# A decoder trunk in fp32 on one core: the query and key projections that fill the attention stage go chunk by chunk to one PSUM bank at a time

## Chip, cores and metric

One core of a Trainium2 chip runs the kernel. The metric is the device time of one execution in microseconds (us). The median of 3 runs counts.

## What is computed

A trunk of two layers is applied to 1024 prompt tokens and 8 sample tokens (T = 1032 columns; model width 1024). Layer 0 mixes with a recurrent block (RG-LRU), layer 1 with sliding-window attention; behind each mixer stands a squared-ReLU MLP. The change lies in the attention of layer 1. Cut to that, the reference reads:

```python
q, k, v = jnp.split(x @ w_qkv, [Q_DIM, Q_DIM + KV_DIM], axis=-1)
q = rms_norm(q.reshape(n, t, N_KV, GROUP, HEAD_DIM), q_g)     # 16 query heads of 64
k = rms_norm(k.reshape(n, t, N_KV, HEAD_DIM), k_g)            # 4 key heads of 64
...
s = jnp.einsum('...qkgd,...skd->...kgqs', q, k).astype(jnp.float32) * (HEAD_DIM ** -0.5)
s = s - alibi_slopes()[:, :, None, None] * dist.astype(jnp.float32)
s = jnp.where(mask, s, NEG_INF)                               # window of 128
m = jnp.maximum(jnp.max(s, axis=-1, keepdims=True), sink)
e = jnp.exp(s - m)
p = e / (jnp.sum(e, axis=-1, keepdims=True) + jnp.exp(sink - m))
return jnp.einsum('...kgqs,...skd->...qkgd', p.astype(v.dtype), v)
```

## The kernel before, in words

Every large product is made of three passes over split operands (`passes`, L235): high part by high part, high by low, low by high, all added up in PSUM. Activations lie with the model width on the 128 partitions, as eight tiles of 1032 columns; `hs[k]` is the pair (`hh`, `hl`) of tile k.

The program runs through the recurrent block, the first MLP, the attention, and the second MLP. In the attention stage (1039.5 to about 1260 us of the trace) the work is written as a loop of NJ = 64 steps j, each one pair of heads' tile t (8 of them) and one block b of 128 queries (8 of them). A step has these parts:

- `stage_a(j)`, called two steps ahead: POOL builds two bias tiles (L955), PE makes four score matmuls into a bank `S` (L961), DVE the masked minimum (L965, twice), ACT the exponentials (L968, twice), DVE the reciprocals (L970), POOL the scaling (L973, twice).
- `stage_b(j)`: PE transposes the probabilities into the bank `T` (L983, up to four), and ACT or DVE, by turns, copies them to `pt` (L988).
- `stage_c(k)`, every fourth step: 28 or 32 matmuls of probabilities by values into the bank `O` (L1005), which ACT and DVE copy out.

These parts leave PE idle, so a generator, `filler` (L1100), puts pieces of other products between them: `take(n)` runs n pieces. The pieces are the query projections t = 1 to 7, with the projection of the second key tile ahead of t = 4, and after step J0 = 52 the output projection. Weights of the next projection are split into `wh` (ACT, L185) and `wl` (DVE, L186) when a projection starts. PSUM has 8 banks: one `N`, three `P`, two `S`, one `T`, one `O`.

A projection has three chunks of columns: 384, 384 and 264 for a query tile, three times 344 for a key tile. In `proj_steps` (L877) all three chunks are summed side by side, in the three `P` banks. A piece is one pass of one of the eight `k`, so three matmuls with the same weights, one to each bank: 24 pieces. Then comes a piece in which all three banks are taken out, and three pieces with the statistics, one for each chunk. These four have no matmul of a projection. So a projection has 28 pieces, and the eight of them 224.

Taking out a chunk of queries is `q_take` (L798): ACT squares it (L805) and writes the high part `hi` (L806), DVE writes the low part `lo` (L807), and SP starts four DMAs to the tiles `q0` and `q1` that the scores read. `q_stats` (L819) makes the sums of squares: 16 small matmuls into bank `N` (L829), a copy by ACT (L832), two transposes (L836), and the factors (L791 to L796); it acts when it is called with the third chunk. For the key tile it is `take_out` (L764) and `k_evac` (L854), which holds the norm (`qk_norm`, with one matmul into `N`, L773) and the split.

The order is that of the calls, as each engine runs its instructions in the order in which they were issued to it. Some matmuls are tied to their place by `issue_after`. `T0 = 24` pieces are taken ahead of the loop, 7 behind each of the first two `stage_a`, then TF = 3.6 in each step on average (three or four) up to step 52. `done` holds the projections that are finished; the loop takes pieces until the tile that `stage_a` needs is in it. From step 46 on `split_o` splits the attention's results into `oh` and `ol` (L276, L277), in tiles that earlier held `hh` and `hl`, and `ensure` splits the first weights of the output projection. At the end of the stage the output projection's `entry_steps` adds the residual on DVE (`y`, L384), starts a DMA from ACT (L385), and scales (L387).

Of the kernel before, what the change touches and what calls it, by code (L numbers as in the profile page):

```python
# [16 lines left out]
P = 128  # L17
D = 1024
M8 = D // P
# [4 lines left out]
NCH = 3  # L24
# [10 lines left out]
KCOLS = [slice(c * CH, (c + 1) * CH) for c in range(NCH)]  # L35
QCOLS = [slice(0, 3 * P), slice(3 * P, 6 * P), slice(6 * P, T)]
# [28 lines left out]
def trunk(ctx: ExitStack, tc: tile.TileContext, I, O):  # L65
# [48 lines left out]
    def B(tag=None):  # L114
        if tag is None:
            tag = ring[turn[0] % len(ring)]
            turn[0] += 1
        return psum["pool"].tile([P, 512], F32, tag=tag, bufs=BANKS[tag], name=nm("b" + tag))
# [11 lines left out]
    def r_(x):  # L130
        return x.bitcast(F32R)
# [103 lines left out]
    def passes(w, x):  # L235
        (wh, wl), (xh, xl) = w, x
        return ((wh, xh), (wh, xl), (wl, xh))
# [508 lines left out]
    def attention(hs):  # L746
# [72 lines left out]
        def q_stats(t, c, s):  # L819
            stq.setdefault(t, []).append(s)  # L820
            if c < 2:
                return
            st, ss, chain = B("N"), stq.pop(t), last.get("values")
            for b in (6, 7, 0, 1, 2, 3, 4, 5):
                r, j = divmod(b, 4)
                with ExitStack() as x:
                    if chain:
                        x.enter_context(tc.issue_after(chain))
                    chain = pe.matmul(st[32 * j:32 * j + 32, r * P:r * P + P], lhsT=blk[:, 0:P:4], rhs=ss[b // 3][:, b % 3 * P:b % 3 * P + P],  # L829
                                      start=True, stop=True).ins  # L830
            sb = S("sts", 256)
            act.copy(sb, st[:, 0:256])  # L832

            def rest():
                for r in range(2):
                    pe.transpose(st[:, 256 + r * P:256 + r * P + P], sb[:, r * P:r * P + P], ident)  # L836
                sums = st[:, 256:512].rearrange("p (b x) -> p b x", x=32)[:, :, 0:32:16]
                y, x, q = (fac[t % 3][:, 2 * NB * k:2 * NB * k + 2 * NB].rearrange("p (b u) -> p b u", u=2) for k in range(3))
                factors_of(y, x, sums, q)

            if t:
                rest()
            return rest

        stats0 = []

        def q_evac(t, c, ps):
            s = q_take(t, c, ps)
# [17 lines left out]
                    for half in (lower, upper):  # L866
                        sp.dma_start(kst[p][u][n][half, cs(c)], x[own, :])

        done = {("q", 0), ("k", 0)}

        def after_values():
            s = ExitStack()
# [1 line left out]
                s.enter_context(tc.issue_after(last["values"]))  # L874
            return s

        def proj_steps(tag, w, cols, take, evac):  # L877
            ps = [B("P")[:, :sl.stop - sl.start] for sl in cols]
            for k in range(M8):
                for a, (wt, xt) in enumerate(passes(w, hs[k])):  # L880
                    for c, sl in enumerate(cols):
                        with after_values():
                            last["mm"] = pe.matmul(ps[c], lhsT=r_(wt[:, k * P:k * P + P]), rhs=r_(xt[:, sl]),  # L883
                                      start=(k == 0 and a == 0), stop=(k == M8 - 1 and a == 2)).ins
                    yield
            sx = [take(c, o) for c, o in enumerate(ps)]
            yield
            for c in range(NCH):
                evac(c, sx[c])
                yield  # L890
            done.add(tag)

        v_tiles = [W("v") for _ in range(2)]
        vnew = tc.dram_tile([2, D], F32, name="vnew")
# [205 lines left out]
        def filler():  # L1100
            for t in range(1, 8):
                if t == 4:
                    yield from proj_steps(("k", 1), unit("k", 1, 1), KCOLS, lambda c, o: take_out(o), lambda *a: k_evac(1, *a))
                yield from proj_steps(("q", t), unit("q", t, 1 if t < 7 else 0), QCOLS, lambda *a, t=t: q_take(t, *a),
                                      lambda *a, t=t: q_stats(t, *a))

        def split_o(t, sl):
            if t not in ohl:
# [19 lines left out]
        def take(n):  # L1128
            for _ in range(n):
                next(fill, None)  # L1130

        NJ = 8 * NB
        WHEN = (44, 47, 49, 54, 60)
        AHEAD, T0, T1, TF, J0, JS = 2, 24, 7, 3.6, 52, 46
        take(T0)
        for j in range(AHEAD):
            stage_a(j)
# [1 line left out]
        for j in range(NJ):  # L1139
            if j + AHEAD < NJ:  # L1140
                while ("q", STEPS[j + AHEAD][0]) not in done:
                    take(1)
                stage_a(j + AHEAD)
            if j == J0:
                run(fill)
                xs, need, grow, fill = out_proj("wo1", srcs, spill, "g_mlp1", None, spill1, before=between, after=ahead(1), early=WAVE)
            if JS <= j < JS + 6:
                split_o(j - JS, cs(0))
            if j in WHEN:
                ensure(index["wo1", WHEN.index(j)])  # L1150
            if j == J0 + 5:
                grow(2)
            if J0 + 4 <= j < J0 + 7:
                split_o(j - J0 - 4, slice(CH, SEQ))
            n = int((j + 1) * TF) - int(j * TF) if j < J0 else 3 if j < J0 + 8 else 4
            take(n // 2)
            if j % 4 == 0 and j > 0:
                stage_c(j // 4 - 1)
            stage_b(j)
            take(n - n // 2)  # L1160
        take(4)
        stage_c(NJ // 4 - 1)
        for t in range(3, 6):
# [417 lines left out]
```

## Time and profile before

| | |
|---|---|
| times of three runs | 2006.60, 2006.76, 2008.14 us; median 2006.76 us |
| the profiled execution | 2005.53 us, of which the span of the trace is 2003.3 us |
| granted TensorE clock, mean | 0.996 |
| busy share of the span | PE 99%, DVE 69%, ACT 52%, POOL 19% |
| matmuls | 15452 |

The profile is of one execution. A row of the windows view gives a stretch of the span, its length, the busy time of each engine in it with the number of instructions that started there, the clock that TensorE was granted (1.00 is full speed), and how busy the DMA engines were. A row of the timeline is an instruction or a run of like ones: start, duration, engine, line, operation, `out<-in`, and in square brackets how long the engine was idle ahead of it and whose instruction released it. A row of the waits view sums such idle times for a pair: the total, how often, and the longest. PE is TensorE, DVE the vector engine, ACT the scalar engine, POOL is GpSimd; names of tiles begin with b for PSUM banks (`bP`, `bS`).

### The profile page before, as it was taken

What the parts mean: (1) busy time and instruction counts of PE and PEld (TensorE: products, weight loads), DVE (VectorE), ACT (ScalarE), POOL (GpSimd) and SP (SyncE); (2) the same over time, 40 slices, a digit from 0 to 9 for tenths busy, and PEclk for the clock granted to TensorE, in tenths of its full rate; (3) what the DMA queues carried; (4) which work ended last, traced back from release to release, by engine and by line L of the source; (5) the groups of instructions that cost most, each with busy time, mean ns of one, the idle gap of its engine ahead of it and who ended that gap; (6) DMA issues with size and microseconds to landing.
All of it is one profiled execution on the core that took longest, in us unless ns stands there. A gap on an engine that the chain in (4) does not pass through costs nothing.

```text
span 2003.3 us, 39287 instructions
## 1 busy us (share of the span) xinstructions
PE 1985.7 (99%) x15452; PEld 1955.7 (98%) x15452; DVE 1385.8 (69%) x2515; ACT 1050.4 (52%) x2049; POOL 373.0 (19%) x688
## 2 busy tenths in 40 slices
PE   9999999999999999999999989999999999999999
PEld 9999999999999999999999979999999999999999
DVE  7986639866676876766746657578766668776673
ACT  8786436444344655545446656455444446554551
POOL 2230100000002133312006657000000002332220
PEclk9999999999999999999999999999999999999999
DMA  5112422434346688769332323623443446877775
GB/s 175 49 43 64 145 82 71 162 130 160 132 148 236 168 231 239 213 164 216 113 100 73 90 70 102 216 82 112 143 154 134 158 138 198 239 208 185 211 194 133
DMA packets 110856, 294.40 MB, mean 147 GB/s; under 512 B 18488, under 2 KB 43328, under 8 KB 110672
## 3 DMA queue, kind: packets, MB, share of 16 engines
q1 hardware_dynamic: 53712, 125.82, 20.4%
q0 software_dynamic: 29024, 97.85, 19.0%
q10 hardware_dynamic: 27936, 68.23, 9.4%
q8 instruction: 121, 1.98, 0.4%
q14 instruction: 63, 0.52, 0.1%
HBM read 170.97 MB, written 108.19 MB: 139 GB/s over the span
## 4 chain that ended last, share of the span: by engine, by line
PE 96%; DMA 1%; DVE 1%; ACT 1%; issue 1%; POOL 0%; ACTq 0%; SPq 0%; DVEq 0%; POOLq 0%
PE bD L557 61%; PE bP L245 11%; PE bS L245 7%; PE bP L883 4%; PE bO L245 3%; PE bT L245 3%; PE bO L1005 1%; PE bS L961 1%; PE bT L983 1%; PE bS L906 1%; DMA tl<-hsum 1%; ACT se L968 0%; DMA spill<-y 0%; PE bN L829 0%; DMA x<-xT 0%
## 5 line engine op out<-in xcount | busy, mean ns | idle before, releaser
L557 PE MATMUL bD<-op,op 128*128 128x258 f32 x5544 | 678.7, 283 | 0.0
L557 PEld LDWEIGHTS bD<-op,op 128*128 128x128 f32 x5544 | 671.2, 189 | 5.0 <-ACT ho L692 4.5
L557 PE MATMUL bD<-tl,op 128*128 128x258 f32 x4704 | 579.6, 284 | 0.3 <-DVE ho L696 0.3
L557 PEld LDWEIGHTS bD<-tl,op 128*128 128x128 f32 x4704 | 570.2, 189 | 7.0 <-ACT ho L692 5.6
L571 POOL DMA_DIRECT2D tl<-hsum x196 | 113.0, 671 | 940.0 <-ACT op L424 414.9
L425 DVE TENSOR_TENSOR op<-ws,op 128x384 fp32r<-128x384 f32 (+2 forms) x288 | 172.4, 606 | 94.2 <-ACT op L424 94.0
L692 ACT COPY he<-bD 128x516 f32<-128x516 f32 x144 | 84.9, 590 | 276.4 <-PE bD L557 276.3
L424 ACT CAST op<-ws 128x384 fp32r<-128x384 f32 (+2 forms) x288 | 158.5, 555 | 109.5 <-PE bD L557 71.1
L692 ACT COPY ho<-bD 128x516 f32<-128x516 f32 x144 | 84.9, 589 | 192.4 <-PE bD L557 192.4
L431 DVE TENSOR_TENSOR tl<-tl 128x516 fp32r<-128x516 f32 x196 | 129.6, 690 | 74.5 <-ACT tl L430 74.4
L424 ACT CAST op<-raw 128x384 fp32r<-128x384 f32 (+2 forms) x216 | 116.9, 556 | 42.7 <-PE bD L557 19.9
L425 DVE TENSOR_TENSOR op<-raw,op 128x384 fp32r<-128x384 f32 (+2 forms) x216 | 127.7, 604 | 5.5 <-ACT op L424 1.5
L700 DVE TENSOR_TENSOR ho<-bD,ho 128x516 f32<-128x516 f32 x72 | 49.9, 693 | 108.0 <-PE bD L557 108.0
L430 ACT CAST tl<-tl 128x516 fp32r<-128x516 f32 x196 | 116.9, 627 | 6.2 <-DMA tl<-hsum 4.7
L968 ACT ACTIVATE se<-se,den 128x257 f32<-128x257 f32 (+1 forms) x128 | 63.3, 496 | 57.0 <-DVE den L965 45.2
L965 DVE CUSTOM_DVE_ANT_0 se<-bS,bias,nsink 128x256 f32<-128x256 f32 (+1 forms) x128 | 63.3, 522 | 32.3 <-PE bS L961 28.9
L186 DVE TENSOR_TENSOR wl<-raw,wh 128x1024 fp32r<-128x1024 f32 (+1 forms) x54 | 63.8, 1190 | 22.3 <-ACT wh L185 13.1
L696 DVE TENSOR_TENSOR ho<-bD,ho 128x516 f32<-128x516 f32 x72 | 49.7, 690 | 39.5 <-ACT ho L692 39.5
L955 POOL TENSOR_SCALAR bias<-con,fac 128x256 f32<-128x256 f32 (+1 forms) x128 | 64.0, 503 | 38.7 <-DVE den L965 27.5
L711 POOL DMA_DIRECT2D spill<-ho x32 | 28.5, 892 | 208.1 <-DVE ho L700 206.2
L973 POOL TENSOR_SCALAR se<-se,den 128x256 f32<-128x256 f32 (+1 forms) x128 | 61.5, 493 | 22.4 <-DVE den L970 20.8
L694 DVE TENSOR_TENSOR he<-bD,he 128x516 f32<-128x516 f32 x72 | 49.7, 690 | 21.0 <-PE bD L557 15.5
(399 smaller groups left out, 3664.0 us busy)
## 6 DMA issues: line engine op xcount, KB each, us to landing
tl<-hsum POOLq DMA_DIRECT2D x196, 258.0 KB, 6.3
raw<-w_up SPq DMA_DIRECT2D x64, 512.0 KB, 4.0
raw<-w_dn SPq DMA_DIRECT2D x72, 384.0 KB, 6.2
spill<-he POOLq DMA_DIRECT2D x32, 516.0 KB, 9.8
spill<-ho POOLq DMA_DIRECT2D x32, 516.0 KB, 6.9
hsum<-ho ACTq DMA_DIRECT2D x28, 516.0 KB, 2.7
hsum<-he ACTq DMA_DIRECT2D x28, 516.0 KB, 2.7
hsum<-ts ACTq DMA_DIRECT2D x28, 516.0 KB, 3.1
```

Source lines behind the costliest of these rows:

```text
L186: eng.tensor_tensor(r_(lo[:, sl]), raw[:, sl], hi[:, sl], ALU.subtract)
L245: last["mm"] = pe.matmul(o, lhsT=r_(wt[:, col(k):col(k) + P]), rhs=r_(xt[:, cs(c)]), start=(k == 0 and a == 0), stop=(k == nk - 1 and a == ...
L424: act.copy(r_(t[:, 0:n]), src)
L425: dve.tensor_tensor(r_(t[:, n:2 * n]), src, t[:, 0:n], ALU.subtract)
L430: act.copy(r_(hi), lo)
L431: dve.tensor_tensor(r_(lo), lo, hi, ALU.subtract)
L557: ins = pe.matmul(d[:, 512 * b:512 * b + QT], lhsT=r_(wt[:, j * P:j * P + P]), rhs=r_(xt[:, QT * b:QT * b + QT]), start=first and j == 0 a ...
L571: pool.dma_start(t[:, n:2 * n], src)
L692: last["copy"] = act.copy(t, f).ins
L883: last["mm"] = pe.matmul(ps[c], lhsT=r_(wt[:, k * P:k * P + P]), rhs=r_(xt[:, sl]), start=(k == 0 and a == 0), stop=(k == M8 - 1 and a == ...
L955: pool.tensor_scalar(bias2[:, o + 256 - n:o + 256], distM[:, 256 - n:256], f[:, 2 * NB + 2 * b + u:2 * NB + 2 * b + u + 1], 0.25 * SLOPES[ ...
L965: dve.tensor_tensor_reduce(se[:, u, 256 - n:256], s[:, u * 256:u * 256 + n], bias2[:, o - n:o], scale=f[:, 2 * b + u:2 * b + u + 1], scala ...
```

## The change

It has three parts, all in the filling pieces.

1. `proj_steps` now goes chunk by chunk. One bank `P` is taken for a chunk, and a piece is one `k` with its three passes into this bank: 8 pieces for a chunk, 24 for a projection, 192 in all. The number of matmuls and their shapes stay as they were.
2. When a chunk is done, it is taken out at once. What follows it (`q_stats` or `k_evac`) is put off: into the list `due[2]`, which is emptied ahead of the piece `k = 2` of the chunk behind it; the second half of `q_stats` (`rest`, the transposes and factors) and the entry into `done` go to `due[5]`, ahead of the piece `k = 5`. After the last projection what is left in the lists is run at once.
3. TF is 3.0 instead of 3.6, so each step has three pieces, one ahead of `stage_b` and two behind it. `stage_c` stands at the end of a step, behind the pieces, where it stood ahead of `stage_b`.

```diff
             if t:
-                rest()
+                due[5].append(rest)
+                due[5].append(lambda: done.add(("q", t)))
             return rest
-        stats0 = []
+        stats0, due = [], {2: [], 5: []}
...
-        done = {("q", 0), ("k", 0)}
+        done = {("q", 0)}
...
-        def proj_steps(tag, w, cols, take, evac):
-            ps = [B("P")[:, :sl.stop - sl.start] for sl in cols]
-            for k in range(M8):
-                for a, (wt, xt) in enumerate(passes(w, hs[k])):
-                    for c, sl in enumerate(cols):
+        def proj_steps(w, cols, take, evac):
+            for c, sl in enumerate(cols):
+                o = B("P")[:, :sl.stop - sl.start]
+                for k in range(M8):
+                    while k in due and due[k]:
+                        due[k].pop(0)()
+                    for a, (wt, xt) in enumerate(passes(w, hs[k])):
                         with after_values():
-                            last["mm"] = pe.matmul(ps[c], lhsT=r_(wt[:, k * P:k * P + P]), rhs=r_(xt[:, sl]),
-                                      start=(k == 0 and a == 0), stop=(k == M8 - 1 and a == 2)).ins
+                            last["mm"] = pe.matmul(o, lhsT=r_(wt[:, k * P:k * P + P]), rhs=r_(xt[:, sl]),
+                                                   start=(k == 0 and a == 0), stop=(k == M8 - 1 and a == 2)).ins
                     yield
-            sx = [take(c, o) for c, o in enumerate(ps)]
-            yield
-            for c in range(NCH):
-                evac(c, sx[c])
-                yield
-            done.add(tag)
+                due[2].append(lambda c=c, sx=take(c, o): evac(c, sx))
...
+            for k in due:
+                while due[k]:
+                    due[k].pop(0)()
...
-        AHEAD, T0, T1, TF, J0, JS = 2, 24, 7, 3.6, 52, 46
+        AHEAD, T0, T1, TF, J0, JS = 2, 24, 7, 3.0, 52, 46
...
             take(n // 2)
+            stage_b(j)
+            take(n - n // 2)
             if j % 4 == 0 and j > 0:
                 stage_c(j // 4 - 1)
-            stage_b(j)
-            take(n - n // 2)
```

The line numbers behind the diff's first hunk move a little: the projections' matmul is L883 before and L886 now, the scores' L961 and L959, the transposes' L983 and L981.

The first place is where one query projection ends and the next begins (t = 5 to t = 6), on PE. Before, these rows followed the last matmul of t = 5 and four scores; `bP_13686`, `bP_13687` and `bP_13688` are the three banks of t = 6, and `sq_13628`, `sq_13608` and `sq_13618` the squares of the chunks of t = 5:

```order
L983 MATMUL bT_13640<-con,se_11337 128x128 x4
L961 MATMUL bS_13646<-kh_12912,q_13271 128x256
L961 MATMUL bS_13646<-kl_12913,q_13271 128x256
L961 MATMUL bS_13646<-kh_12914,q_13272 128x256
L961 MATMUL bS_13646<-kl_12915,q_13272 128x256
L883 MATMUL bP_13686<-hh_10733,wh_13366 128x384
L829 MATMUL bN_13661<-sq_13628,con 32x128 x2
L829 MATMUL bN_13661<-sq_13608,con 32x128 x3
L829 MATMUL bN_13661<-sq_13618,con 32x128 x3
L883 MATMUL bP_13687<-hh_10733,wh_13366 128x384
L836 MATMUL bN_13661<-con,sts_13670 128x128 x2
L883 MATMUL bP_13688<-hh_10733,wh_13366 128x264
```

Now the last matmul of t = 5 is followed by four transposes, by the first matmul of t = 6, and then by these rows; `bP_13652` is the bank of the first chunk of t = 6, and `sq_13634` the square of the last chunk of t = 5:

```order
L886 MATMUL bP_13652<-hl_10734,wh_13307 128x384
L886 MATMUL bP_13652<-hh_10733,wl_13308 128x384
L886 MATMUL bP_13652<-hh_10735,wh_13307 128x384
L886 MATMUL bP_13652<-hl_10736,wh_13307 128x384
L886 MATMUL bP_13652<-hh_10735,wl_13308 128x384
L959 MATMUL bS_13659<-kh_12737,q_13090 128x256
L959 MATMUL bS_13659<-kl_12738,q_13090 128x256
L959 MATMUL bS_13659<-kh_12739,q_13091 128x256
L959 MATMUL bS_13659<-kl_12740,q_13091 128x256
L829 MATMUL bN_13674<-sq_13634,con 32x128 x2
L829 MATMUL bN_13674<-sq_13433,con 32x128 x3
L829 MATMUL bN_13674<-sq_13516,con 32x128 x3
```

The small matmuls L829 stood behind four transposes, four or eight scores and one matmul of the next projection, whose bank had to be taken out first; now four transposes, six matmuls into a bank that has been free for a chunk, and four scores lie between them and the end of the chunk that they need, and the transposes L836 follow a good way further on. The squares of the first two chunks were made one and two chunks earlier.

The second place is near the end of the stage, on ACT. Before, its queue held these rows one behind the other; `y_14846` is a sum with the residual, and `wh_14855` and `wh_14861` are high parts of weights of the output projection:

```order
L385 DMA spill_2510<-y_14846 128x344
L296 ACTIVATE sq_14849<-y_14846 128x344
L387 ACTIVATE x_14844<-y_14846,vec 128x344
L185 CAST wh_14855<-raw_14698 128x1024
L185 CAST wh_14861<-raw_14853 128x1024
```

Now it reads as follows, with two more sums, `y_14828` and `y_14837`, and a copy of probabilities between:

```order
L185 CAST wh_14855<-raw_14698 128x1024
L385 DMA spill_2510<-y_14828 128x344
L986 COPY pt_14800<-bT_14814 128x512
L296 ACTIVATE sq_14831<-y_14828 128x344
L387 ACTIVATE x_14826<-y_14828,vec 128x344
L385 DMA spill_2510<-y_14837 128x344
L296 ACTIVATE sq_14840<-y_14837 128x344
L387 ACTIVATE x_14835<-y_14837,vec 128x344
L385 DMA spill_2510<-y_14846 128x344
L296 ACTIVATE sq_14849<-y_14846 128x344
L387 ACTIVATE x_14844<-y_14846,vec 128x344
L185 CAST wh_14861<-raw_14853 128x1024
```

The cast of `wh_14855` moved from behind `y_14846` to a place ahead of `y_14828`; that of `wh_14861` stays behind `y_14846`.

The third place is on ACT, near the end of the last projection (t = 7), in the changed kernel alone. `oh_14201` and `oh_14264` are high parts of attention results in tiles that held `hh` or `hl`, `bP_14129` is the bank of the second chunk of t = 7, `bT_14277` a bank of transposes:

```order
L805 ACTIVATE sq_14216<-bP_14129 128x384
L966 ACTIVATE se_11337,den_11327<-se_11337,den_11327 128x257 x2
L276 CAST oh_14201<-o_13027 128x344
L806 ACTIVATE hi_14217<-bP_14129,qg 128x384
L276 CAST oh_14201<-o_13027 128x680
L1008 COPY o_14042<-bO_14230 128x256
L276 CAST oh_14264<-o_13360 128x344
L966 ACTIVATE se_11337,den_11328<-se_11337,den_11328 128x257
L986 COPY pt_14211<-bT_14277 128x512
```

The tile of `oh_14201` is free when the third chunk of t = 7 no longer reads the `hh` or `hl` that lay there. Before, the three chunks read each of these tiles side by side, so the first tiles were free early in the projection; now every tile is read until its `k` in the third chunk, which are the last 8 of 24 pieces. The rows behind `oh_14201` wait in ACT's queue with it.

More of the change, by code (lines that the diff above doesn't have):

```diff
@@ L1102, in filler @@
                 if t == 4:
-                    yield from proj_steps(("k", 1), unit("k", 1, 1), KCOLS, lambda c, o: take_out(o), lambda *a: k_evac(1, *a))
-                yield from proj_steps(("q", t), unit("q", t, 1 if t < 7 else 0), QCOLS, lambda *a, t=t: q_take(t, *a),
+                    yield from proj_steps(unit("k", 1, 1), KCOLS, lambda c, o: take_out(o), lambda *a: k_evac(1, *a))
+                yield from proj_steps(unit("q", t, 1 if t < 7 else 0), QCOLS, lambda *a, t=t: q_take(t, *a),
                                       lambda *a, t=t: q_stats(t, *a))
+            for k in due:
+                while due[k]:
+                    due[k].pop(0)()
         def split_o(t, sl):
```

## The prediction

> **What bounds the kernel now.** I read the page first. TensorE is busy in nearly the whole span, so a change that leaves its matmuls as they are can only win idle time, or time at a lower clock:
>
> ```profile
> PE 1985.7 (99%) x15452; PEld 1955.7 (98%) x15452; DVE 1385.8 (69%) x2515; ACT 1050.4 (52%) x2049; POOL 373.0 (19%) x688
> ```
>
> 1985.7 of 2003.3 us leaves 17.6 us idle. The windows view tells where. Its first row is the part of the attention stage with the filling projections, the second and third the part with the output projection:
>
> ```profile
> 1039.50:1226.00 186.50, 177.01 (x1477) 166.20 (x1477) 114.14 (x390) 113.33 (x352) 117.46 (x273) 0.97 0.28 73
> 1226.00:1260.00 34.00, 34.00 (x301) 32.50 (x297) 23.06 (x73) 22.02 (x66) 19.20 (x47) 1.00 0.51 169
> 1260.00:1275.00 15.00, 12.75 (x89) 11.62 (x88) 7.64 (x12) 7.54 (x12) 0.00 (x0) 0.89 0.79 243
> ```
>
> In the first row PE lacks 186.50 − 177.01 = 9.5 us, and its clock is 0.97; in the third it lacks 2.25 us at 0.89. No other engine is near its full time there (DVE 114 of 186.5 us, ACT 113, POOL 117), so PE waits for single late results, not for an engine's throughput. Which ones, the waits view says for PE between 1039.5 and 1275 us (total, times, longest):
>
> ```profile
> PE bP L883 <- DVE lo L807: 4.0, 2, 2.1
> PE bN L829 <- ACT sq L805: 2.6, 2, 1.4
> PE bP L245 <- ACT wh L185: 2.2, 1, 2.2
> PE bO L1005 <- ACT pt L988: 1.3, 1, 1.3
> PE bS L961 <- PE bS L961: 0.5, 1, 0.5
> PE bP L245 <- DVE lo L807: 0.5, 1, 0.5
> PE bT L983 <- POOL se L957: 0.4, 1, 0.4
> ```
>
> Two ends of a projection make 4.0 + 2.6 = 6.6 us of the 9.5. This is one of them on PE's timeline (the last bracket of a row: idle before it, and for whom); the first rows are the rhythm between:
>
> ```profile
> 1162.81 0.60 PE L983 MATMUL bT<-con,se 128*128 128x128 f32 x4
> 1163.16 0.72 PE L883 MATMUL bP<-hl,wh 128*128 128x384 f32 x3
> 1163.72 0.64 PE L883 MATMUL bP<-hh,wl 128*128 128x384 f32 x3
> 1164.20 0.28 PE L961 MATMUL bS<-kh,q 128*128 128x256 f32 x1
> 1164.67 0.60 PE L983 MATMUL bT<-con,se 128*128 128x128 f32 x4
> ...
> 1167.82 0.45 PE L883 MATMUL bP<-hh,wh 128*128 128x384 f32 x1 [2.07 <-DVE lo L807]
> 1169.62 1.05 PE L829 MATMUL bN<-sq,con 128*32 128x128 f32 x16 [1.36 <-ACT sq L805]
> ```
>
> All three banks end at 1164.2 us. The next projection needs the first of them when it has just been filled, and DVE has other work ahead of the taking out: the split of the next weights and four of the softmax's operations, which stand between the low parts:
>
> ```profile
> 1164.92 1.39 DVE L186 TENSOR_TENSOR wl<-raw,wh 128x1024 fp32r<-128x1024 f32 x1 [0.71 <-ACT wh L185]
> 1166.23 0.53 DVE L965 CUSTOM_DVE_ANT_0 se<-bS,bias,nsink 128x256 f32<-128x256 f32 x1
> 1167.16 0.60 DVE L807 SCALAR_TENSOR_TENSOR lo<-bP,qg,hi 128x384 fp32r<-128x384 f32 x1
> 1168.95 0.61 DVE L807 SCALAR_TENSOR_TENSOR lo<-bP,qg,hi 128x384 fp32r<-128x384 f32 x1
> ```
>
> Each long gap costs a second time. The windows of 2 us behind the two ends, and behind the gap at 1264 us, show a granted clock of 0.50 (the number ahead of the last two):
>
> ```profile
> 1170.00:1172.00 2.00, 2.00 (x19) 1.11 (x9) 0.88 (x4) 0.87 (x4) 0.94 (x2) 0.50 0.85 235
> 1172.00:1174.00 2.00, 2.00 (x27) 1.96 (x28) 0.64 (x3) 0.63 (x3) 0.37 (x1) 0.70 0.63 152
> 1198.00:1200.00 2.00, 1.76 (x18) 1.23 (x19) 1.03 (x5) 1.42 (x5) 0.18 (x1) 0.50 0.86 200
> 1200.00:1202.00 2.00, 2.00 (x15) 1.75 (x16) 0.41 (x2) 0.70 (x3) 0.93 (x2) 0.50 0.68 160
> 1202.00:1204.00 2.00, 2.00 (x22) 1.92 (x19) 0.23 (x1) 0.00 (x0) 0.72 (x2) 0.52 0.42 106
> 1264.00:1266.00 2.00, 1.80 (x9) 1.77 (x10) 1.23 (x1) 1.09 (x2) 0.00 (x0) 0.84 0.77 239
> 1266.00:1268.00 2.00, 2.00 (x8) 2.00 (x8) 0.00 (x0) 0.00 (x0) 0.00 (x0) 0.50 0.69 200
> 1268.00:1270.00 2.00, 2.00 (x27) 1.63 (x28) 0.08 (x1) 0.00 (x0) 0.00 (x0) 0.81 1.02 316
> ```
>
> Busy time at a clock c loses 1 − c of itself: 1.00 + 0.60 + 0.88 + 1.00 + 0.96 = 4.4 us at the two ends, so 2.2 us for each, and 0.29 + 1.00 + 0.38 = 1.7 us at the third. The gaps of up to 1.3 us cost nothing beside themselves; the windows that hold the 0.5 us wait for `bS` and the 1.3 us wait for `pt` stay at 1.00:
>
> ```profile
> 1050.00:1060.00 10.00, 9.46 (x75) 8.72 (x74) 5.67 (x24) 6.39 (x22) 5.63 (x13) 1.00 0.39 94
> 1140.00:1150.00 10.00, 8.71 (x90) 7.99 (x89) 7.26 (x25) 8.24 (x26) 4.39 (x12) 1.00 0.54 129
> ```
>
> So what can be won: 9.5 + 4.4 = 13.9 us among the projections, and 2.25 + 1.7 = 3.9 us at the stage's end, together 17.8 us.
>
> **The change part by part.** *One bank at a time.* Matmuls, weight loads and shapes stay the same in number. A piece of three takes as long in one bank as in three, if the adding up in one bank costs nothing: the nearest row is the output projection below, whose 344-wide matmuls into one bank stand 0.16 us apart (1264.46 to 1264.62), against (1163.72 − 1163.16) / 3 = 0.19 and (1164.20 − 1163.72) / 3 = 0.16 us for three matmuls in three banks. I take zero. What goes is the wait for a bank just filled: with three banks, a chunk begins in a bank that was taken out a chunk of 24 matmuls earlier, about 3.8 us at 0.16 us each even without the rest between. The waits `bP L883 <- DVE lo` (4.0) go, also where DVE does the 1.39 us split first.
>
> *Sums later.* Before, three squares had to be made in a row, and only scores, transposes and one stalled matmul lay ahead of L829; now two of the squares are long made, and four transposes, six matmuls and four scores lie between. By the rhythm rows these take 0.35 + (0.56 + 0.48) + 0.47 = 1.9 us. ACT needs for the square 0.48 us, behind one exponential pair or one `hi`:
>
> ```profile
> 1164.79 0.48 ACT L805 ACTIVATE sq<-bP 128x384 f32<-128x384 f32 x1
> 1165.17 0.57 ACT L806 ACTIVATE hi<-bP,qg 128x384 fp32r<-128x384 f32 x1
> ```
>
> That is 1 to 2 us, so mostly covered; without that cover each wait is up to 1.4 us, as in the row of L829 above. I leave 1.0 us in all for the seven ends and the key's three norms (ends 0 and 2.6, what there is now; I take a value nearer to 0, as only the squares of the last chunk can be late). The transposes L836 follow several us behind the copy they need.
>
> *Three pieces in every step, values last.* 3.6 pieces a step, one in seven of which (4 of 28) had no matmul of a projection, become 3. PE then does the same amount in each four steps, and the wait for `pt` (1.3), which came as L1005 stood soon behind the copy, goes: two pieces of 0.5 us now lie between the transposes and the values. `pt` and `bO` stay in use a piece or two longer; nothing in front of PE needs them sooner.
>
> *SP.* The four DMAs of a chunk are issued when it ends, no longer 12 in a row; the scores that read them come later than before relative to the first chunks, and one chunk's own at the same distance. I cost this at nothing; the cover is the 10 pieces or more up to the scores.
>
> *What is late next.* The tiles of `hh` and `hl` are now read to the end of the last projection, as each chunk passes over all eight. Attention results that are split into these tiles (`oh`, `ol`) wait in ACT's and DVE's queues, with `hi`, exponentials and a copy of probabilities behind them. Behind the last chunk of t = 7 only four matmuls of 0.16 us lie ahead of L829, as the lists are run at once there. Before, this place cost the last two rows of the waits, 0.5 + 0.4 = 0.9 us. Its low end is that; its high end is what a boundary costs now, 2.07 + 1.36 us idle and 2.2 us of clock, 5.6 us. I take 2.5 us: PE's waits there are for L829, for a group of transposes and for a matmul, each one ACT operation (0.5 to 1 us) behind, so nearer to the low end, and short of the gaps that lose the clock. The 0.5 us for `bS` at the start stays, as the 24 pieces ahead of the loop still end there.
>
> *The stage's end.* There PE waited 2.2 us for weights whose cast stood on ACT behind a sum that waited for its DMA:
>
> ```profile
> 1261.33 0.52 DVE L384 TENSOR_TENSOR y<-bP,x 128x344 f32<-128x344 f32 x1 [2.19 <-DMA spill<-y]
> ...
> 1262.25 0.49 ACT L296 ACTIVATE sq<-y 128x344 f32<-128x344 f32 x1 [1.07 <-DVE y L384]
> ...
> 1263.12 1.98 ACT L185 CAST wh<-raw 128x1024 fp32r<-128x1024 f32 x2
> ...
> 1264.46 0.32 PE L245 MATMUL bP<-ol,wh 128*128 128x344 f32 x1
> 1264.62 0.32 PE L245 MATMUL bP<-oh,wh 128*128 128x344 f32 x1
> ```
>
> The first of the two casts now stands three sums earlier. Between it and the need for the second PE has 24 + 12 + 12 matmuls of 0.16 us, 7.7 us, which is more than the 2.19 us by which DVE and the 1.07 us by which ACT were late. I leave 0.7 us; ends 0 and the old 3.9.
>
> **Sum.** Of 17.8 us, 0.5 + 1.0 + 2.5 + 0.7 = 4.7 stays, 13.1 goes. The profiled execution, 2005.53 us, would become 1992.4; it lies 1.2 us below the median of the three runs, which becomes 2006.76 − 13.1 = **1993.7 us**. About 0.2% (4 us) is what a measurement of this kernel can tell from no change.
>
> **The rivals.** *Many short stalls in place of few long ones (slower).* There are now 24 takings out, each tied to one moment, and a chunk's last square is needed 1.9 us on. If each makes PE wait, the point that decides is 13.9 / 24 = 0.6 us; at 1.0 us each the stage loses 24.0 instead of 13.9, and with 3.2 won at the end the time is 2006.76 + 10.1 − 3.2 = 2013.7 us. Against it: in this row the key projection's norms and evacuations ran chunk by chunk among matmuls of the next projection, and PE had no idle time:
>
> ```profile
> 1120.00:1130.00 10.00, 10.00 (x67) 9.25 (x66) 9.09 (x28) 8.63 (x26) 8.12 (x15) 1.00 0.39 110
> ```
>
> Chance 0.06.
>
> *Short stalls that lose the clock (slower).* If each change of banks lets the clock fall, it costs 2.2 us each, 24 × 2.2 = 53 us in place of 13.9, and the time is 2006.76 + 39 − 3.2, about 2043 us. Gaps of 0.5 and 1.3 us left the clock at 1.00 in the two rows of 10 us, so a gap would have to be about 2 us for that, and banks were changed with no gap at all before. The Trainium skill, "TensorE: Matmul & The Clock Gate", section "A second HAM failure mode: psum-queue depth-cycling", speaks against the change here: it tells of a kernel that cycles through PSUM banks, whose TensorE idles shortly between groups often enough that its clock swings between half and full. By that page the change would be this rival; the trace so far does not agree, with clock 1.00 behind gaps of up to 1.3 us. Chance 0.02.
>
> *The late tiles block the queues.* If ACT or DVE waits for a tile of `hh` longer than I worked out, a gap of over 2 us follows around steps 46 to 54, and the clock falls: 5.6 us in place of 2.5, the gain is 10.0, the time 1996.8 us; with a second such gap 11.2 in place of 2.5, 2002.4 us. For it: ACT has three splits and the last projection's evacuation to do in the same few steps. Against: PE's work there does not depend on these splits for some steps. Chance 0.22.
>
> *The bank was not the cause.* If the two long gaps come from a backlog of ACT and DVE (the weights' split of 1.39 us on top of the softmax) and not from the bank's order, PE meets it at the next scores or transposes: 2 × (2.07 + 1.36) + 4.4 = 11.3 us stay, 2.6 + 3.2 − 2.5 = 3.3 are won, 2003.5 us. For it: the scores too waited in DVE's queue behind the split (1.39 us from 1164.92). Against: DVE at 61% and ACT at 61% of the first window catch up within a step. Chance 0.08.
>
> That the change does not do what it says is no rival: the rows of the two orders show the matmuls moved.
>
> **How the numbers follow.** The forecast has 0.62, with a range of its own from 1990.4 (nothing left at the sums, 0.9 at the late tiles, none at the end: 1.0 + 1.6 + 0.7 = 3.3 more) to 1997. The four rivals have 0.06, 0.02, 0.22 and 0.08. Faster by over 0.2%: 0.62 + 0.22, less 0.02 for the second gap, which with its 2002.4 lies at the bound, so 0.82. Within 0.2%: 0.08 + 0.02 = 0.10. Slower: 0.06 + 0.02 = 0.08. A range from 1990 to 2002 holds the forecast and nearly all of the blocked queues, 0.8.
>
> **What would show it.** Right: PE idle of 2 to 5 us and a clock of 1.00 in the stage; no wait `bP L886 <- DVE lo`; waits of L829 for `sq` of under 0.5 us each; the wait for `wh` L185 gone; the matmuls as dense as before. The forecast is wrong in the first step if L886 still waits for `lo`, in the second if L829 waits over 1 us at each end, in the fourth if gaps over 2 us with clock 0.50 stand near the last projection's end, and in the sum if the projections' matmuls stand farther apart than 0.16 us.

## The result, and the profile after

The changed kernel takes 1993.05 us (median of 6 runs, 1991.73 to 1993.58), the kernel before 2006.68 us (6 runs, 2005.91 to 2008.14). The ratio is 0.993, with a 95% interval from 0.9917 to 0.9943. That is 13.6 us less; 13.1 were forecast, and 1993.7 us. The profiled executions say the same: 2005.53 and 1991.73 us, 13.8 us apart.

The page's line of busy times, then the windows of the attention stage, which is 13 us earlier at its end than before:

```profile
PE 1980.5 (100%) x15452; PEld 1950.6 (98%) x15452; DVE 1384.9 (70%) x2515; ACT 1050.3 (53%) x2049; POOL 375.2 (19%) x688
```

```profile
1039.50:1213.00 173.50, 172.18 (x1479) 161.55 (x1478) 112.10 (x381) 113.77 (x351) 116.19 (x267) 1.00 0.31 80
1213.00:1247.00 34.00, 31.56 (x270) 29.34 (x270) 21.87 (x76) 20.32 (x63) 21.98 (x53) 1.00 0.39 128
1247.00:1262.00 15.00, 15.00 (x118) 14.54 (x117) 11.80 (x21) 10.70 (x19) 0.35 (x2) 1.00 1.00 314
```

PE now lacks 1.32 us in the first stretch and 2.44 in the second, 3.8 us in all where it lacked 9.5 + 2.25 = 11.7, and the clock is 1.00 throughout where 0.97 and 0.89 stood: the 6.1 us that the lower clock cost are gone. Idle time saved and clock regained make 8.0 + 6.1 = 14.1 us, the span shrank by 13.3. PE's waits in the stage, all of them:

```profile
PE bT L981 <- POOL se L971: 2.6, 4, 1.1
PE bP L245 <- DVE ol L1013: 0.6, 1, 0.6
```

In this view no wait for `lo`, `sq` or `wh` is left; instead the transposes wait four times for POOL's scaling of the probabilities. The end of a projection (t = 3 to the second key tile) on PE's timeline:

```profile
1090.92 0.28 PE L886 MATMUL bP<-hh,wl 128*128 128x264 f32 x1
1091.05 0.60 PE L981 MATMUL bT<-con,se 128*128 128x128 f32 x4
1091.40 0.41 PE L886 MATMUL bP<-hh,wh 128*128 128x344 f32 x1
...
1092.99 0.67 PE L829 MATMUL bN<-sq,con 128*32 128x128 f32 x16
...
1094.62 1.00 PE L981 MATMUL bT<-con,se 128*128 128x128 f32 x4 [0.28 <-POOL se L971]
```

The next projection's first matmul follows at once, L829 comes 2 us after the chunk's end without a wait, and the first wait is a new one, behind it.

### The profile page after: what moved, and what is told of

It is laid out like the page before. It is cut to its first block, busy times and chain, and to the rows that moved or that the text cites. A ratio compares the mean times of both kernels' runs of the same rounds, so it can differ in the third digit from the quotient of the medians.

```text
span 1990.0 us, 39281 instructions
## 1 busy us (share of the span) xinstructions
PE 1980.5 (100%) x15452; PEld 1950.6 (98%) x15452; DVE 1384.9 (70%) x2515; ACT 1050.3 (53%) x2049; POOL 375.2 (19%) x688
## 4 chain that ended last, share of the span: by engine, by line
PE 96%; POOL 1%; DVE 1%; DMA 1%; issue 0%; ACT 0%; ACTq 0%; SPq 0%; DVEq 0%; POOLq 0%
PE bD L557 61%; PE bP L245 11%; PE bS L245 7%; PE bP L886 4%; PE bT L245 3%; PE bO L245 3%; PE bS L959 1%; PE bO L1003 1%; PE bT L981 1%; PE bS L904 1%; DMA tl<-hsum 1%; POOL bias L953 0%; POOL se L971 0%; DMA x<-xT 0%; DVE se L963 0%
## 5 line engine op out<-in xcount | busy, mean ns | idle before, releaser
L886 PE MATMUL bP<-hh,wh 128*128 128x384 f32 (+2 forms) x192 | 67.3, 351 | 0.0
```

Of the source, the lines that this page charges most:

```text
L886: last["mm"] = pe.matmul(o, lhsT=r_(wt[:, k * P:k * P + P]), rhs=r_(xt[:, sl]), start=(k == 0 and a == 0), stop=(k == M8 - 1 and a == 2)).ins
```

## The experiments

Two theories stood against each other. The bank theory, that of the prediction: the long waits came from banks that were needed when they had just been filled. The backlog theory: they came from what ACT and DVE had to do at a projection's end, the split of the next weights above all, and three even pieces in a step cure it. The medians and ratios below are against runs of the kernel before on the same chip (2006.4 to 2006.9 us).

**The sums issued at once.**

```diff
-                due[5].append(rest)
-                due[5].append(lambda: done.add(("q", t)))
+                rest()
+                done.add(("q", t))
...
-                due[2].append(lambda c=c, sx=take(c, o): evac(c, sx))
+                evac(c, take(c, o))
```

> The changed kernel, but the sums of squares, their transposes and the factors are issued as soon as a chunk is taken out, with no matmul of the next chunk between. The bank theory (the long waits came from banks that were needed when just filled; putting off the sums covers the square and the copy): L829 waits 0.5 to 1.4 us for sq and L836 0.4 to 1 us for the copy of the sums, at seven ends, about 2 us each, and where the two together reach 2 us the clock falls: about 2007 us, between 2000 and 2018. The backlog theory (the long waits came from what ACT and DVE had to do at a projection's end, the split of the next weights above all, and three even pieces in a step cure it): 1993 to 1996 us.

It took 1994.48 us (ratio 0.9938, 0.9922 to 0.9955), 1.4 us above the changed kernel, with overlapping intervals. That is what the backlog theory forecast, and outside the range of the bank theory. Short waits show better in the waits of the weight loads (PEld), which stand ahead of each matmul, since the ends of matmuls are modelled. First this run's, then the changed kernel's:

```profile
PEld bT L981 <- POOL se L971: 4.2, 9, 1.7
PEld bN L829 <- ACT sq L805: 3.0, 7, 0.6
```

```profile
PEld bT L981 <- POOL se L971: 5.7, 10, 1.3
...
PEld bN L829 <- ACT sq L805: 0.2, 1, 0.2
```

The sums wait 2.8 us more, the transposes behind them 1.5 us less; the difference of 1.3 us is near the 1.4 us of the times. The bank theory's size was wrong here: with one bank for a chunk only one square is fresh, so each wait is 0.4 us on average and not 0.5 to 1.4, the transposes L836 do not wait, and the clock holds.

**The values early.**

```diff
             take(n // 2)
+            if j % 4 == 0 and j > 0:
+                stage_c(j // 4 - 1)
             stage_b(j)
             take(n - n // 2)
-            if j % 4 == 0 and j > 0:
-                stage_c(j // 4 - 1)
```

> The changed kernel, but the values (stage_c) stand ahead of the transposes and the second half of the pieces, as before the change. Bank theory: three pieces and the scores, 1.9 us, still lie between the last transposes and the values, the copy takes 0.6 us, so at most one wait of 1.3 us comes back: 1993 to 1995 us. Backlog theory: the same, the place of the values is no cause by either; a result above 1997 us would say that the place matters by itself.

It took 1994.21 us (0.994, 0.9926 to 0.9955; four runs, 1993.13 to 1997.89), as expected by both. But the profile shows something that neither expected; PE's waits:

```profile
PE bP L245 <- ACT wh L185: 2.6, 1, 2.6
PE bT L981 <- POOL se L971: 1.6, 2, 1.1
```

The loss at the stage's end is back. On ACT the cast that PE waits for (1251.82 us) runs behind the square of a late sum (1250.95 us) again, as in the kernel before. So it is the place of the values that moved the cast; the changed kernel's gain at the stage's end belongs to this part. No wait for `pt` came back, so it was not the late values that took that one away.

**Three banks again.** The pieces, the put-off sums and the late values stay as changed.

```diff
+            ps = [B("P")[:, :sl.stop - sl.start] for sl in cols]
+            for k in range(M8):
+                while k in due and due[k]:
+                    due[k].pop(0)()
+                for a, (wt, xt) in enumerate(passes(w, hs[k])):
+                    for c, sl in enumerate(cols):
...
+                    yield
+            for c, o in enumerate(ps):
+                due[2].append(lambda c=c, sx=take(c, o): evac(c, sx))
```

> The changed kernel with its even pieces, its put-off sums and its late values, but with three banks side by side again, all taken out at a projection's end. Bank theory: the waits for lo come back, about 2.1 us at two or more of the seven ends, with the clock at 0.5 behind those that reach 2 us: 1997 to 2003 us. Backlog theory: even pieces are enough: 1993 to 1995 us.

It took 2034.12 us: 41 us above the changed kernel, and slower than the kernel before (1.0138, 1.0123 to 1.0153). PE's waits, and a stretch behind one of the projections' ends:

```profile
PE bP L886 <- DVE aux L811: 10.9, 5, 4.1
PE bP L886 <- DVE lo L807: 7.6, 7, 2.3
PE bT L982 <- POOL se L972: 4.1, 7, 1.0
```

```profile
1074.00:1076.00 2.00, 0.43 (x3) 0.11 (x1) 0.20 (x2) 0.15 (x2) 1.11 (x3) 1.00 0.69 171
1076.00:1078.00 2.00, 1.23 (x7) 0.99 (x9) 0.70 (x3) 0.00 (x0) 0.00 (x0) 0.81 0.56 136
1078.00:1080.00 2.00, 2.00 (x20) 2.00 (x21) 0.00 (x0) 0.00 (x0) 0.00 (x0) 0.50 0.41 104
```

The ends now wait for `lo` and, at the third bank, for its last reader (L811), up to 4.1 us, and clock 0.50 follows. The page gives PE 2000.3 us busy in a span of 2032.2: 31.9 us idle, 22.4 more than the changed kernel's 9.5, and 19.8 us more busy time with the same matmuls. By the prediction's working (busy time times 1 − c, here in windows of 2 us) the clock took 11.5 us of these; the rest fits waits inside groups of matmuls, which count as busy: by the weight loads the three waits come to 31.2 us, by PE to 22.6. The backlog theory falls, the bank theory was right in kind and forecast far too little: it had counted on two bad ends, as in the kernel before, where the four pieces without matmuls of a projection still stood between. That these four pieces were the cover is likely, but no run tests it alone.

**The kernel before, weights split in the middle of a projection.**

```diff
+        def halfway(steps, name):
+            for n, _ in enumerate(steps):
+                if n == 12 and name:
+                    ensure(index[name])
+                yield
```

`filler` runs each projection through it, with the next projection's name, and takes its own weight with `unit("q", t, 0)`, so that no projection's weight is split at its start. The splits of the output projection's weights, at the steps of `WHEN`, stay.

> The kernel before, but each next weight is split 12 pieces into a projection and not at its start, so ACT's 1.03 us and DVE's 1.39 us no longer stand at a projection's end. Bank theory: the first lo comes 1.4 us earlier, the two waits for lo fall from 2.0 to about 0.7 us, those of L829 for sq (1.3 us) stay, and the clock perhaps holds: 1999 to 2004 us. Backlog theory: both kinds of wait go, with the clock: about 1996 us.

It took 2006.77 us (1.000, 0.999 to 1.0009): no change. PE's waits for `lo`, then PE and DVE at the two ends:

```profile
PE bP L883 <- DVE lo L807: 4.2, 3, 2.0
```

```profile
1165.03 0.64 PE L883 MATMUL bP<-hh,wl 128*128 128x384 f32 x3
...
1167.89 0.44 PE L883 MATMUL bP<-hh,wh 128*128 128x384 f32 x1 [0.84 <-DVE lo L807]
1169.75 0.45 PE L883 MATMUL bP<-hh,wh 128*128 128x384 f32 x1 [1.41 <-DVE lo L807]
...
1197.28 0.44 PE L883 MATMUL bP<-hh,wh 128*128 128x384 f32 x1 [1.95 <-DVE lo L807]
```

```profile
1167.23 0.61 DVE L807 SCALAR_TENSOR_TENSOR lo<-bP,qg,hi 128x384 fp32r<-128x384 f32 x1
...
1194.48 1.23 DVE L186 TENSOR_TENSOR wl<-raw,wh 128x1024 fp32r<-128x1024 f32 x1 [0.62 <-ACT wh L185]
```

At the first end (t = 5) no split stands in DVE's queue. `lo` starts 2.2 us after the projection's last piece (1165.03 us), where it was 3.4 us in the prediction's rows (1163.72 to 1167.16), and PE's first wait falls from 2.07 to 0.84 us, near the 0.7 of the bank theory. But the second bank is now waited for as well, 1.41 us, and the copy for L836, 0.54 us. Together this is 2.8 us where 2.07 + 1.36 = 3.4 us stood, and the clock falls to 0.50 again. At the second end (t = 6) the split is still there: it is that of the output projection's first weight, at step 44, which this edit leaves in place, and the wait is 1.95 us where it was 1.96. So the split made the first wait at an end long, but without it the wait moves to the next of the three banks that are taken out in a row. What both ends would do without a split no run shows.

**The kernel before with one bank for a chunk**, and no other part of the change:

```diff
+            sx = []
+            for c, sl in enumerate(cols):
+                o = B("P")[:, :sl.stop - sl.start]
+                for k in range(M8):
+                    for a, (wt, xt) in enumerate(passes(w, hs[k])):
...
+                    yield
+                sx.append(take(c, o))
             yield
             for c in range(NCH):
                 evac(c, sx[c])
                 yield
```

> The kernel before with the first part of the change alone: each chunk is summed in one bank and taken out when it is done; the empty piece, the three pieces with the sums, 3.6 pieces in a step and the early values stay. Bank theory: the waits for lo (4.0 us) go, and with them the drops of the clock (4.4 us); of the 2.6 us of L829 at most half stays, as only one square is late; the loss at the stage's end (3.9 us) stays: 1995 to 1999 us. Rival (the bank alone does little, the even pieces do it): 2003 to 2006 us.

It took 1993.77 us (0.9933, 0.9917 to 0.9949), better than expected and within the changed kernel's interval. PE's waits in the stage:

```profile
PE bP L245 <- ACT wh L185: 2.8, 1, 2.8
PE bO L1006 <- ACT pt L989: 1.3, 3, 0.5
```

No wait for `lo`, none for `sq`, none for POOL. The loss at the stage's end is there (2.8 us). So the first part alone gives all of the measured gain, and the other two parts take with one hand (the waits for POOL) what they give with the other (the stage's end).

**The kernel before with an earlier cast.**

```diff
-        WHEN = (44, 47, 49, 54, 60)
+        WHEN = (44, 47, 49, 54, 60, 62)
```

> The kernel before, with a sixth weight of the output projection split at step 62, so that its cast stands ahead of the sums with the residual on ACT. If the cast's place is the cause of the loss at the stage's end, the wait of 2.2 us for wh and the clock's 1.7 us go: 2002.5 us, between 2001.5 and 2004. If the sums and their DMAs would hold PE there anyway, another wait takes its place: 2006 us.

It took 2004.26 us (0.9987, 0.9978 to 0.9997), 2.7 us less, just above the range that was expected. The cast's place was the cause; two shorter waits came in its place, by the view of PE's waits:

```profile
PE bS L245 <- DVE wl L186: 0.7, 1, 0.7
...
PE bS L245 <- ACT wh L185: 0.4, 1, 0.4
```

They are for the next weight, whose cast still stands behind the sums: 3.9 − 1.1 = 2.8.

**The changed kernel, one cast later.**

```diff
-        WHEN = (44, 47, 49, 54, 60)
+        WHEN = (44, 47, 49, 55, 60)
```

> The changed kernel, with the fourth weight of the output projection split one step later (55 and not 54), so that its cast and subtraction no longer stand among the factors of t = 7. If these made the factors late, and through POOL's biases the scaling of the probabilities, the 1.9 us of PE idle near 1225 us go: about 1991.2 us. If POOL is late by its own work: 1993 us.

It took 1991.13 us (0.992, 0.9907 to 0.9933; 5 runs, none above 1991.48, where the changed kernel had none below 1991.73). The ratio's interval overlaps that of the changed kernel, so it is the waits that tell: the two of 0.78 and 1.09 us near 1225 us are gone; the others stay, by PE's and by the weight loads' waits:

```profile
PE bT L981 <- POOL se L971: 0.7, 2, 0.4
```

```profile
PEld bT L981 <- POOL se L971: 3.9, 10, 0.8
```

**Both splits later in the changed kernel**: the cast as in the run before, and `halfway` for the projections' weights.

> As the run before, and each next projection's weight is split 12 pieces into a projection instead of at its start. If the splits at a projection's end make the two waits of the transposes (0.3 and 0.4 us) there, 1990.5 us; if not, the same as the run before.

It took 1987.81 us (0.9904, 0.989 to 0.9918; 4 runs, none above 1988.91): 5.2 us below the changed kernel's median, below what was expected, and the fastest of all. The same edit that did nothing in the kernel before took 3.3 us from the run ahead of it. The window of the stage up to 1213 us, and the weight loads' waits for POOL:

```profile
1039.50:1213.00 173.50, 173.45 (x1498) 164.27 (x1497) 115.25 (x390) 117.30 (x357) 119.09 (x272) 1.00 0.32 83
```

```profile
PEld bT L981 <- POOL se L971: 0.9, 3, 0.3
```

PE is idle for 0.05 us in 173.5. Why 3.3 us and not the 0.7 us of PE's waits: a group of four transposes that waits inside counts as busy (1.00 us at 1094.62 where 0.60 is usual). By the weight loads the waits for POOL were 3.9 us in 10 places in the run ahead and are 0.9 here, 3.0 us less.

**One bank alone with the later splits.** The kernel before, with the edits of the fifth and the fourth experiment, and `WHEN = (44, 47, 49, 55, 60, 62)`.

> The kernel before with one bank for a chunk (the first part of the change alone), and the splits moved: the projections' weights 12 pieces into a projection, the output projection's fourth weight at step 55, its sixth at step 62. If the put-off sums, the even pieces and the late values are needed for the best time, 1991 us or more, as waits of L829 or L836 remain at the projections' ends; if they are not, the 2.8 us for wh go and it comes to 1988 to 1990 us, beside the 1987.8 of the run with all parts.

It took 1993.35 us (0.9935, 0.9921 to 0.9948), no better than the one bank alone. That is the first of the two forecasts, but not by the waits that it named, L829 and L836. The 2.8 us for `wh` went, and others came or stayed:

```profile
PE bT L984 <- POOL se L974: 1.7, 1, 1.7
...
PE bS L245 <- DVE wl L186: 0.7, 1, 0.7
PE bO L1006 <- ACT pt L989: 0.6, 2, 0.4
```

So the later splits pay nothing with the first part alone, and 5.2 us with all three: the other two parts are needed for the best time, though they add nothing measurable to the first part as long as the splits stay where they were.

**Both splits later, the sums at once**: the edit of the first experiment on the eighth.

> The run with both later splits, without the put-off sums: they are issued as soon as a chunk is taken out. If putting off is worth what the first run of this kind showed (1.4 us beside the changed kernel, with 1.1 us of waits of L829 for sq), about 1989 us; if the splits at the projections' ends made those waits, 1988 us.

It took 1990.50 us (0.9919, 0.9906 to 0.9933), 2.7 us above the eighth (on another chip, where the kernel before took 0.3 us less), more than forecast by either. The weight loads' waits:

```profile
PEld bN L829 <- ACT sq L805: 2.3, 7, 0.6
...
PEld bT L981 <- POOL se L971: 0.9, 3, 0.4
```

The waits for POOL stay at 0.9 us, and those for the square come on top. With the other waits away, the putting off is worth what it covers. But without it the later splits still took 4.0 us (1994.48 us in the first experiment, 1990.50 here). So what they need most is the even pieces or the late values; no run separates these two.

## Why the prediction was right

*The bank.* Right in kind, and shown from both sides: one bank alone gives the whole gain, three banks with all the rest lose 41 us. The working held that the waits for `lo` (4.0 us) and the clock behind them (4.4 us) go, and they went. Its account of why `lo` was late put DVE's split of 1.39 us first. Where the fourth experiment took the split away `lo` came 1.2 us sooner, but the wait moved to the second bank and the time stayed; at the other end the split was one of the output projection's. Nothing in the sum hung on that. The rival "the bank was not the cause" falls by the third and the fifth experiment: even pieces did not cure the waits, and one bank did, with the split at the projection's end still there. What these two do not separate is the second effect of the same edit: the three takings out no longer stand in a row in the queues of ACT and DVE.

*The sums.* 1.0 us was left for the waits of L829; it was 0.2. The price given for the lost cover, up to 1.4 us for each wait, is the term that was mis-sized most: 3.0 us in 7 places, 0.6 at the longest. That price was read from a boundary where three squares stood in a row, and one bank for a chunk had already done away with that.

*Even pieces, late values.* The wait for `pt` went as forecast, and stayed away with the values early (second experiment). That the late values would also move a cast at the stage's end was read from the order of ACT but not tied to them; the second experiment ties it.

*The late tiles.* 2.5 us were left for the last projection's end, and 1.9 us came near 1225 us (0.78 and 1.09): near in size, by the wrong path, so that is luck. The prediction named L829, a group of transposes and a matmul, each behind an ACT operation of the late tiles. It was the factors of t = 7. On ACT the cast stands between two steps of them, DVE's subtraction ahead of the next:

```profile
1217.38 0.20 ACT L792 ACTIVATE fac<-fac 128x16 f32<-128x16 f32 x1
1217.49 1.03 ACT L185 CAST wh<-raw 128x1024 fp32r<-128x1024 f32 x1
1218.42 0.21 ACT L793 ACTIVATE fac<-fac 128x16 f32<-128x16 f32 x1
```

```profile
1218.55 1.22 DVE L186 TENSOR_TENSOR wl<-raw,wh 128x1024 fp32r<-128x1024 f32 x1 [0.87 <-ACT wh L185]
1219.70 0.22 DVE L794 SCALAR_TENSOR_TENSOR fac<-bN,vec,fac 128x16 f32<-128x16 f32 x1
...
1220.99 0.22 DVE L796 SCALAR_TENSOR_TENSOR fac<-bN,vec,fac 128x16 f32<-128x16 f32 x1
```

```profile
1221.52 2.53 POOL L953 TENSOR_SCALAR bias<-con,fac 128x128 f32<-128x128 f32 x6
1224.03 2.59 POOL L971 TENSOR_SCALAR se<-se,den 128x256 f32<-128x256 f32 x4
```

```profile
1224.35 1.23 DVE L186 TENSOR_TENSOR wl<-raw,wh 128x1024 fp32r<-128x1024 f32 x1
```

POOL could not build the biases of t = 7 before 1221 us, six of them stood ahead of the scaling in its queue, and PE waited for that up to 1224.56 us. The second wait, up to 1225.98 us, had one more cause: the second of the four scalings took 1.44 us (1224.48 to 1225.92) where 0.48 is usual, beside the next subtraction on DVE, the last row (more on this at the end). The seventh experiment moved the cast at 1217 us, the scalings began 1.2 us sooner, and the two waits went.

*The stage's end.* 0.7 us were left, none is there. That 3.9 us could be had by the cast's place alone is not quite so: 2.7 in the sixth experiment.

*The start.* The 0.5 us for `bS` was to stay and went: the window from 1040 to 1060 us is full.

*What no term held.* Two waits for POOL at other places (0.28 us at 1094.62 and 0.43 us at 1143.57) and 0.56 us for `ol` in the output projection at 1244.73 us. By the weight loads the transposes waited 5.7 us for POOL in all. PE's idle time, on which the prediction's sum was built, does not show half of that; the eighth experiment took most of it away.

In sum 4.7 us were left and 3.8 are there. Four terms came out 0.5 to 1.0 us too large and the waits that no term held make up 1.3 us of that, so that the sum is as near as it is is partly luck. Neither slower rival came: with 24 takings out PE was idle for 3.8 us in all, far below the 0.6 us each at which they would decide, and the clock stayed at 1.00. The Trainium skill, "TensorE: Matmul & The Clock Gate", section "A second HAM failure mode: psum-queue depth-cycling", tells of a clock that swings because a kernel cycles through PSUM banks and idles shortly between groups of matmuls. The changed kernel cycles through its banks too, without such idle times and at clock 1.00; the 0.50 at 1078 us in the third experiment came behind a wait of 2.34 us at a projection's end. So no run here shows the case of that section. What differs between these two kernels is the time from a bank's last matmul to its next first one.

## What to carry to other kernels

When an engine fills several buffers side by side, they all come full at one time, and the next group must wait for the slowest chain behind the first of them; filled one after the other, each has the others' time to be emptied, at the same number of instructions. Read what stands in the queue ahead of the late instruction, but take it away once before it is called the cause, and look at every place whether it is gone and where the wait went. And when a bottleneck goes, try the edits again that did nothing before: the later splits were worth nothing in one kernel and, together with a later cast, 5.2 us in the other.

## What the hardware did that was not expected

*The clock behind a gap.* Gaps of much the same length had different ends. In the fifth experiment PE waited 2.83 us, up to 1253.08, and the clock held; in the fourth it waited 2.66 us, up to 1265.89, for the same cast, and lost it. The windows around and behind each gap, the fifth's first:

```profile
1251.00:1253.00 2.00, 0.00 (x0) 0.00 (x0) 0.76 (x3) 1.86 (x4) 0.00 (x0) 1.00 1.12 358
1253.00:1255.00 2.00, 1.92 (x12) 1.84 (x13) 1.23 (x1) 0.98 (x2) 0.00 (x0) 1.00 0.34 112
1255.00:1257.00 2.00, 2.00 (x23) 1.78 (x23) 0.00 (x0) 0.00 (x0) 0.00 (x0) 1.00 0.70 242
```

```profile
1265.00:1267.00 2.00, 1.11 (x7) 1.11 (x8) 1.07 (x1) 1.79 (x2) 0.00 (x0) 1.00 0.96 298
1267.00:1269.00 2.00, 2.00 (x9) 1.94 (x8) 0.15 (x1) 0.00 (x0) 0.00 (x0) 0.52 0.39 107
```

The gap of 2.15 us in the kernel before lost it too. So length alone does not decide between 2.1 and 2.8 us. Nor must one gap be about 2 us long, as the prediction worked out: at the first end of the fourth experiment waits of 0.84, 1.41 and 0.54 us, close together, were followed by this window:

```profile
1172.00:1174.00 2.00, 2.00 (x19) 1.93 (x20) 0.64 (x3) 0.67 (x3) 0.56 (x2) 0.50 0.55 137
```

The Trainium skill, "TensorE: Matmul & The Clock Gate", section "What's actually happening", says that the clock falls after an idle window of about 3.4 us and that the windows run freely; that a gap's place in the window matters would agree with these rows, but no run here moved a gap on purpose, and the full idle window does not agree, as gaps of 2.15 and 2.66 us were enough.

*POOL beside a DVE operation of two inputs.* In the changed kernel a copy of two elements on POOL, usually 0.19 us, took 1.17 us, and it ended when DVE's subtraction did (1092.25 + 1.17 = 1093.42 us and 1092.01 + 1.37 = 1093.38 us):

```profile
1092.25 1.17 POOL L955 COPY se<-nsink 128x2 f32<-128x2 f32 x1
```

```profile
1092.01 1.37 DVE L186 TENSOR_TENSOR wl<-raw,wh 128x1024 fp32r<-128x1024 f32 x1
```

In the changed kernel's stage ten of these subtractions had a POOL operation that started in them. Nine such operations took 1.17 to 1.72 us where 0.19 to 0.48 us is usual, and ended after the subtraction; the tenth started in its last 0.1 us and took 0.19 us. The 22 POOL operations that started in a DVE operation with one input in PSUM (L807, L1013) took their usual time. The Trainium skill, "SBUF — State Buffer", section "SBUF: two separate sides", says that a DVE operation with two inputs in SBUF and a GpSimd operation that reads SBUF lock each other out for a whole instruction; the rows agree.

So the split at a projection's end can delay the scaling on POOL and with it the transposes. It also delays DVE's own reciprocals, on which the scaling waits: the next one starts at 1093.30 us, behind the subtraction. And the cast that belongs to the split stands ahead of ACT's exponentials (1090.18 us). The eighth experiment moved all of this away; no run separates the three.
